# A new operation order for a hybrid transformer block: planner rules and due times changed

## The chip, the cores and the metric

The kernel runs on one core of a Trainium2 chip. The metric is the device time of one execution in microseconds (us); the time before is the median of three runs. A core has five engines that run their own instruction streams side by side: TensorE (PE in the profile, with its weight loads as PEld), VectorE (DVE), ScalarE (ACT), GpSimd (POOL) and SyncE (SP, which here only issues transfers).

## The reference

One layer over 512 tokens of width 1024, all in float32: a norm, one input projection, three groups of attention heads (A: differential attention, 4 heads; B: forgetting attention, 6 heads; C: chunked attention with a relative bias, 6 heads), an output projection into the residual, then a gated MLP with a causal convolution of width 3, and a gated input embedding. Cut to its core:

```python
z = rms_norm(h, ln_mix) @ w_in                       # 1024 -> 3590 columns
q1, q2, k1, k2, va, qf, kf, vf, fg, qc, kc, vc = split(z)
o_a = diff_attention(q1, q2, k1, k2, va, lam, ...)   # softmax - lam * softmax, then a norm per head
o_b = forgetting_attention(qf, kf, vf, log_sigmoid(fg + bias))
o_c = chunk_attention(qc, kc, vc, rel_bias)
h = h + concat(o_a, o_b, o_c) @ w_out
u = rms_norm(h, ln_ffn) @ w_up                       # 1024 -> 2 x 2816
gate, val = split(conv_b + sum(conv_w[j] * shifted(u, j) for j in range(3)))
h = h + (silu(gate) * val) @ w_down
h = h + (p @ w_ple_proj) * sigmoid(rms_norm(h, ln_ple) @ w_ple_gate)
```

## The kernel before

Every float32 product is made of three products of split operands: a matrix is rounded to a high part (`whi`, by ScalarE) and the rest is its low part (`wlo`, mostly by VectorE; some by GpSimd, or by a GpSimd transfer that adds in flight, `wlo<-wraw` on POOL's queue). Weights come from memory into the buffers `wraw` by SP's queue, and in the MLP partly by POOL's, which adds two parts while it loads.

The program has two halves with a plan each: attention (`first`, the class `Plan` with group "first") and the rest (the MLP, its down projection and the gate). The code does not issue an instruction when it is written down. `Plan.add` records it with what it depends on, `Plan.price` gives it a duration, and `Plan.due` gives it a due time: TensorE's operations in the written order follow each other without gaps, and the group that an operation belongs to moves its due time by its entry in the table `SHIFT` (zero when it is absent). Operations of the other engines take their due times from whoever needs them. `Plan.solve` then walks through time: whichever engine can start first takes, among its operations whose inputs are there, the one that is due first. What comes out is the order of instructions on each of the five engines, and `Plan.emit` issues them so; the real waits are semaphores between the engines. A plan's time is a model, and only its order reaches the chip.

Rules of `solve` that matter here:

- TensorE prefers operations whose inputs have been there for `SURE` = 0.1 us.
- A rule on transposes (`turns`, `alone`, `STICK`): TensorE's transposes, through which probabilities, queries, keys and normed tokens pass, are kept in runs. The planner changes between transposes and products only if enough of the other kind is due, and a transpose that stands alone makes the next operation 0.08 us longer.
- Transfers: one `wire` carries SP's and POOL's transfers one after the other.
- `Plan.region` says which bytes an access covers, so that accesses that overlap get a dependency. For the kernel's inputs and output in memory it is one range from the first to the last byte.

Names of groups: `in7_2` is token tile 2 of input projection 7; `B0a` transposes queries and keys of head pair B0, whose halves GpSimd then moves into place (`q<-q`, `q<-ql`, `k<-k`); `B0s0` are the scores of its first head (`s<-k,q`), `B0p0` the transposes of probabilities, `B0v0` the products with the values; `out0_1` is the output projection. In the MLP, `u9_0` is a part of the up projection of column block 9, `s14_1` one of the seven products that a pair of blocks is made of in another way, `dn1_0_t2` a part of the down projection, and `g13_0`, `g13_256` the two halves of the last tile of the gate, whose results go to memory by the last two stores.

The output is made in `kernel` by

```python
    args["out"] = nc.dram_tensor(f"out_{i}_dram", shape, dt, kind="ExternalOutput").ap()[0]
```

All instructions are recorded through one helper, `now`, so that the profile puts them all on one line, L357; the tiles tell them apart.

Of the kernel before, what the change touches and what calls it, by code (L numbers as in the profile page):

```python
# [41 lines left out]
for _i in range(3):  # L42
# [5 lines left out]
AHEAD = 2  # L48
# [46 lines left out]
STAND_INS = {}  # L95
# [28 lines left out]
class Plan:  # L124
# [5 lines left out]
    def __init__(self, clock, there=(), mem=None, fresh=0.0, late=0.0):  # L130
        self.group, self.loaded, self.fresh, self.late = "first", set(), fresh, late
        self.clock, self.there, self.ops, self.mem = clock, [(v.tensor.name, self.region(v), t) for v, t in there], [], mem or {}

    @staticmethod
    def region(v):
        size = 2 if v.dtype == BF16 else 4
        (row, pn), *rest = [tuple(x) for x in v.ap]
        if v.tensor.space == bass.MemoryType.DRAM and v.tensor.name not in STAND_INS:
            return 0, 1, v.offset * size, (v.offset + (pn - 1) * row + sum((n - 1) * st for st, n in rest) + 1) * size
        p0, c0 = divmod(v.offset, row)  # L140
        return p0, p0 + pn, c0 * size, (c0 + sum((n - 1) * st for st, n in rest) + 1) * size
# [42 lines left out]
    def price(self, op):  # L184
# [4 lines left out]
        op.move, op.turns = 0, op.name == "transpose"  # L189
# [29 lines left out]
    LONG, STICK = 0.6, 2.0  # L219
    HW, SW, AT_ONCE = 0.37e6, 0.105e6, 8  # L220
    SURE, AHEAD, MUCH, WAIT = 0.1, 1.0, 2.0, 0.6
# [14 lines left out]
    def solve(self):  # L236
# [6 lines left out]
        wire, out, order = 0.0, {"sp": [], "pool": []}, []  # L243
        turns, alone = False, False
# [4 lines left out]
        while True:  # L249
# [10 lines left out]
            if e == "pe":  # L260
                can = [q for q in can if q.at + self.SURE <= t] or can
            op = min(can, key=rank)
            if e == "pe" and op.turns != turns:
                same = [q for q in can if q.turns == turns and q.dl < op.dl + self.STICK]
# [58 lines left out]
def kernel(ctx: ExitStack, tc: tile.TileContext, x, xt0, xt, pt_in, small, g_ffn_in, bias_c,  # L323
# [15 lines left out]
    PLAN = []  # L339
# [1718 lines left out]
```

## Time and profile before

| | |
|---|---|
| Time, median of 3 runs | 709.2 us (707.82, 709.2, 709.85) |
| Profiled execution | 707.89 us, span 706.0 us |
| TensorE busy | 690.3 us, 98% of the span, 4420 matmuls |
| VectorE busy | 552.5 us, 78%, 1126 instructions |
| ScalarE busy | 408.7 us, 58%, 781 instructions |
| GpSimd busy | 300.6 us, 43%, 403 instructions |
| Transfers | 92.72 MB, mean 131 GB/s |
| Granted TensorE clock | 0.998 |

The span is from the first to the last instruction; the execution takes a little longer than its span. Shares are of the span. An engine that is not on the chain that ended last may stand idle at no cost; TensorE's idle time is what counts in this kernel. A matmul's duration in the profile is modelled and overlaps the next one, so the distance between starts tells more than the durations. Attention fills the first 280 us or so, the up and down projections go on to about 650 us, and the gate ends the kernel.

### The profile page before, as it was taken

The numbers are of one execution on the slowest core, as the hardware profiler recorded it, in microseconds if no ns is written. First come the engines' busy times: TensorE is split into PE (matmuls) and PEld (weight loads), VectorE is DVE, ScalarE is ACT, GpSimd is POOL, SyncE is SP. The second block draws the span as 40 slices with busy tenths as digits, with TensorE's granted clock in tenths as the row PEclk, the third lists the DMA queues.
The fourth block names the chain that finished last, engine by engine and source line by source line (L and its number), as shares of the span: only waits on it lengthen the run. The fifth ranks groups of instructions, "written<-read, shape, count | busy, mean of one in ns | idle before, by whom it ended". The sixth has DMA issues, their size and how long they took to land.

```text
span 706.0 us, 12402 instructions
## 1 busy us (share of the span) xinstructions
PE 690.3 (98%) x4420; PEld 636.4 (90%) x4420; DVE 552.5 (78%) x1126; ACT 408.7 (58%) x781; POOL 300.6 (43%) x403
## 2 busy tenths in 40 slices
PE   7999999999999999999999999999999999999997
PEld 7999999898999888899998999889988888999886
DVE  7679878879788666789888887997877998878722
ACT  6657676565766575666666435665345674536711
POOL 3788677766665452223223334304432203245200
PEclk9999999999999999999999999999999999999999
DMA  9523444423112252584763278651488552204521
GB/s 321 201 83 111 125 117 128 118 60 109 45 61 76 75 124 83 200 244 105 214 159 113 68 186 207 163 162 33 139 211 209 183 168 82 91 32 155 163 85 46
DMA packets 41275, 92.72 MB, mean 131 GB/s; under 512 B 4694, under 2 KB 7510, under 8 KB 41212
## 3 DMA queue, kind: packets, MB, share of 16 engines
q1 hardware_dynamic: 34572, 78.24, 33.1%
q0 software_dynamic: 6352, 13.38, 10.8%
q8 instruction: 35, 0.57, 0.3%
q10 hardware_dynamic: 288, 0.30, 0.1%
q14 instruction: 28, 0.23, 0.1%
HBM read 83.63 MB, written 4.21 MB: 124 GB/s over the span
## 4 chain that ended last, share of the span: by engine, by line
PE 91%; DVE 3%; DMA 2%; ACT 2%; POOL 1%; issue 1%; ACTq 0%; POOLq 0%
PE z L357 46%; PE s L357 22%; PE t L357 16%; PE o L357 7%; DMA wraw<-in_w_up_dram 1%; DVE wlo L357 1%; POOL k L357 1%; POOL q L357 1%; ACT whi L357 1%; DMA zn<-in_w_in_dram 0%; DVE e L357 0%; DVE conv L357 0%; POOL rs L357 0%; ACT e L357 0%; DVE kl L357 0%
## 5 line engine op out<-in xcount | busy, mean ns | idle before, releaser
L357 ACT CAST whi<-wraw 128x768 fp32r<-128x768 f32 (+2 forms) x140 | 106.1, 768 | 59.9 <-POOL wraw L357 11.4
L357 PE MATMUL z<-whi,Th 128*128 128x384 f32 (+2 forms) x356 | 123.4, 351 | 4.5 <-ACT whi L357 4.5
L357 DVE TENSOR_TENSOR wlo<-wraw,whi 128x768 fp32r<-128x768 f32 (+2 forms) x122 | 111.5, 930 | 15.4 <-ACT whi L357 13.6
L357 PE MATMUL z<-wlo,Th 128*128 128x384 f32 (+2 forms) x356 | 123.0, 350 | 0.0
L357 PE MATMUL z<-whi,Tl 128*128 128x384 f32 (+2 forms) x356 | 121.8, 347 | 0.0
L357 PEld LDWEIGHTS z<-whi,Th 128*128 128x128 f32 x356 | 66.9, 189 | 8.0 <-ACT whi L357 4.5
L357 POOL TENSOR_TENSOR wraw<-wraw,wraw 128x256 f32<-128x256 f32 (+1 forms) x22 | 28.3, 1285 | 101.3 <-DVE wlo L357 53.6
L357 PEld LDWEIGHTS z<-wlo,Th 128*128 128x128 f32 x356 | 67.2, 189 | 4.0 <-DVE wlo L357 0.4
L357 PEld LDWEIGHTS z<-whi,Tl 128*128 128x128 f32 x356 | 67.0, 189 | 3.8
L357 ACT ACTIVATE e<-e,st 128x128 f32<-128x128 f32 (+3 forms) x80 | 44.7, 560 | 29.8 <-DVE st L357 29.4
L357 PE MATMUL z<-Th,whi 128*128 128x512 f32 (+1 forms) x156 | 53.2, 346 | 1.4 <-ACT whi L357 1.3
L357 PE MATMUL s<-Th,whi 128*128 128x512 f32 (+1 forms) x156 | 53.3, 345 | 0.6 <-ACT whi L357 0.6
L357 PE MATMUL s<-Th,wlo 128*128 128x512 f32 (+1 forms) x156 | 53.7, 345 | 0.0
L357 PE MATMUL s<-Tl,whi 128*128 128x512 f32 (+1 forms) x156 | 53.6, 345 | 0.0
L357 PE MATMUL z<-Tl,whi 128*128 128x512 f32 (+1 forms) x156 | 53.5, 344 | 0.0
L357 PE MATMUL z<-Th,wlo 128*128 128x512 f32 (+1 forms) x156 | 53.4, 344 | 0.0
L357 POOL TENSOR_TENSOR rs<-rs,nhalf 128x4 f32<-128x4 f32 x40 | 43.5, 1091 | 4.8 <-DVE rs L357 2.3
L357 DVE CUSTOM_DVE_ANT_0 e<-s,bias 128x128 f32<-128x128 f32 (+3 forms) x74 | 33.7, 469 | 12.4 <-PE s L357 7.2
L357 DVE TENSOR_TENSOR conv<-conv,conv 128x512 f32<-128x512 f32 (+1 forms) x31 | 21.0, 691 | 24.0 <-ACT conv L357 23.8
L357 POOL TENSOR_SCALAR e<-e,st 128x512 f32<-128x512 f32 (+3 forms) x48 | 27.2, 576 | 18.1 <-DVE st L357 16.8
L357 PEld LDWEIGHTS z<-Th,whi 128*128 128x128 f32 x156 | 29.1, 188 | 4.8 <-ACT whi L357 1.8
L357 PEld LDWEIGHTS s<-Th,whi 128*128 128x128 f32 x156 | 29.2, 188 | 3.8 <-ACT whi L357 0.8
(352 smaller groups left out, 2152.4 us busy)
## 6 DMA issues: line engine op xcount, KB each, us to landing
wraw<-in_w_up_dram SPq DMA_DIRECT2D x41, 384.0 KB, 4.3
wraw<-in_w_in_dram SPq DMA_DIRECT2D x28, 384.0 KB, 3.7
wraw<-in_w_down_dram SPq DMA_DIRECT2D x16, 384.0 KB, 3.6
whi_again<-in_w_up_dram SPq DMA_DIRECT2D x11, 384.0 KB, 4.5
wraw<-in_w_out_dram SPq DMA_DIRECT2D x16, 256.0 KB, 2.7
wlo_again<-in_w_up_dram SPq DMA_DIRECT2D x10, 384.0 KB, 4.3
wraw<-in_w_up_dram SPq DMA_DIRECT2D x15, 256.0 KB, 4.1
wlo<-wraw POOLq DMA_DIRECT2D x7, 384.0 KB, 4.2
```

Source lines behind the costliest of these rows:

```text
L357: ins = getattr(self.eng, op)(*a, **k)
```

## The change

Five edits, all in the planner; no instruction of the computation is added or removed.

1. The rule on transposes is gone, in both plans: TensorE takes whatever is due first, and a lone transpose has no extra price.
2. The margin `SURE` becomes an argument: 0.15 in attention, 0.1 in the MLP's plan as before.
3. In attention's plan SP's and POOL's transfers have a wire each. The MLP's plan keeps one (`one_wire=True`).
4. `Plan.region` gives a tensor called `out_dram` a rectangle of rows and columns instead of a range of bytes, so that stores to the same rows and other columns do not overlap.
5. The table `SHIFT` has new values throughout, found by a search over the plan; for the MLP the search was made with disturbed landing and operation times.

The lines of `SHIFT` with the groups that the text below speaks of, and the other edits:

```diff
 SHIFT = {
...
-    "in2_1": 19.7, "A0b": -17.1, "in2_2": -18.9, "A0s01": -25, "A0s02": -5.9, "in2_3": -4.1, "fc": 0.8, "in3_0": 4.7,
...
-    "in4_3": 7.8, "in5_0": 4.2, "A1p0": 3.1, "A1s11": -0.2, "in5_1": -10, "A1s12": 2.3, "in5_2": -3.3, "B0a": -0.2,
-    "A1v0": 16.5, "in5_3": -2.8, "A1p1": -3.7, "in6_0": 20.4, "A1v1": -10.3, "B0s0": -8.5, "B0s1": 4, "B1a": -14.7,
...
-    "u9_0": -22.5, "s8_0": -11.8, "u9_1": 7.5, "s8_1": 22.6, "u9_2": 11.4, "s8_6": -22.9, "s8_2": -6.8, "s8_3": -0.9,
...
-    "s14_6": -0.7, "s14_2": 1.3, "s14_3": 5.5, "u17_0": 0.4, "u17_1": -3.4, "s14_4": -0.2, "s14_5": 1.3,
...
-    "g03_0": 10.9, "g10_0": -7.1, "g11_0": -4.4, "g12_0": 1.2, "g13_0": 6.1, "g13_256": 2.2,
...
+    "in1_1": 0.4, "in1_2": -4.5, "A0a": 0.1, "in1_3": -3.6, "in2_0": -0.9, "in2_1": 1, "A0b": 23.2, "in2_2": -4.2,
+    "A0s01": -13.3, "A0s02": -12.2, "in2_3": -2.1, "fc": 21.6, "in3_0": 3.4, "A0p0": -8.9, "A0v0": 8.1, "in3_1": -1,
...
+    "in5_0": 3.3, "A1p0": 19.6, "A1s11": 1.9, "in5_1": 8, "A1s12": -2.6, "in5_2": -0.4, "B0a": -18.4, "A1v0": 7.8,
+    "in5_3": 4.1, "A1p1": -7.9, "in6_0": 0.7, "A1v1": 15.6, "B0s0": -14.1, "B0s1": 7, "B1a": -18.8, "in6_1": -13.2,
+    "B0p0": 8.5, "B0v0": -4.1, "B1s0": -4.4, "in6_2": -1.5, "B0p1": 1, "B1s1": -2.6, "B0v1": -5.6, "B1p0": -0.1,
...
+    "u9_0": 1.7, "s8_0": 24.8, "u9_1": 12.8, "s8_1": -11.8, "u9_2": -20.9, "s8_6": -2.3, "s8_2": -11.8, "s8_3": 1.7,
...
+    "dn1_1_t4": -18.1, "dn1_1_t1": 12.5, "dn1_1_t2": -2.6, "dn1_1_t3": 16.5, "dn1_1_a2": 12, "u15_0": 12.6,
+    "s14_0": -2.1, "u15_1": 14.7, "s14_1": -0.5, "u15_2": -1.5, "s14_2": 5.9, "s14_3": -19.9, "u17_0": -3.4,
+    "u17_1": 0.2, "u17_2": -12.6, "s16_0": 1.4, "s16_2": -6.5, "s16_3": 3.9, "u19_0": -4.1, "u19_1": -0.5,
...
+    "g10_0": -1.8, "g12_0": -7.5, "g13_0": -2, "g13_256": 2.4,
...
-    def __init__(self, clock, there=(), mem=None, fresh=0.0, late=0.0):
+    def __init__(self, clock, there=(), mem=None, fresh=0.0, late=0.0, sure=0.15, one_wire=False):
+        self.sure, self.one_wire = sure, one_wire
         self.group, self.loaded, self.fresh, self.late = "first", set(), fresh, late
         self.clock, self.there, self.ops, self.mem = clock, [(v.tensor.name, self.region(v), t) for v, t in there], [], mem or {}
 
@@ -135,7 +137,7 @@
     def region(v):
         size = 2 if v.dtype == BF16 else 4
         (row, pn), *rest = [tuple(x) for x in v.ap]
-        if v.tensor.space == bass.MemoryType.DRAM and v.tensor.name not in STAND_INS:
+        if v.tensor.space == bass.MemoryType.DRAM and v.tensor.name not in STAND_INS and v.tensor.name != "out_dram":
             return 0, 1, v.offset * size, (v.offset + (pn - 1) * row + sum((n - 1) * st for st, n in rest) + 1) * size
         p0, c0 = divmod(v.offset, row)
         return p0, p0 + pn, c0 * size, (c0 + sum((n - 1) * st for st, n in rest) + 1) * size
@@ -186,7 +188,7 @@
         n = self.width(op.outs[0])
         cols = sum(1 for v in op.ins if self.width(v) == 1) - (op.name == "reciprocal")
         acc = "accum_out" in k
-        op.move, op.turns = 0, op.name == "transpose"
+        op.move = 0
         if e == "pe":
             if op.name == "transpose":
                 op.busy = 0.109
@@ -216,9 +218,9 @@
         op.port = e == "pool" and not op.move or e == "dve" and (
             len(here) == len(op.ins) and (op.name == "tensor_scalar" or op.name in ("tensor_tensor", "scalar_tensor_tensor")))
 
-    LONG, STICK = 0.6, 2.0
+    LONG = 0.6
     HW, SW, AT_ONCE = 0.37e6, 0.105e6, 8
-    SURE, AHEAD, MUCH, WAIT = 0.1, 1.0, 2.0, 0.6
+    AHEAD, MUCH, WAIT = 1.0, 2.0, 0.6
     SPARE = {"act": 1.02, "dve": 1.02, "pool": 1.05}
     ENGINES = ("dve", "pe", "act", "pool", "sp")
 
@@ -240,8 +242,7 @@
             op.left, op.at = len(op.deps), op.ready + self.LEAD[op.eng.name]
             if not op.left:
                 free[op.eng.name].append(op)
-        wire, out, order = 0.0, {"sp": [], "pool": []}, []
-        turns, alone = False, False
+        wire, out, order = {"sp": 0.0, "pool": 0.0}, {"sp": [], "pool": []}, []
         held = {"dve": 0.0, "pool": 0.0}
         other = {"dve": "pool", "pool": "dve"}
         when = lambda q: max(q.at, held[other[q.eng.name]] + (self.late if q.eng.name == "pool" else 0.0)) if q.port else q.at
@@ -258,12 +259,8 @@
             t, e = best
             can = [q for q in free[e] if when(q) <= t]
             if e == "pe":
-                can = [q for q in can if q.at + self.SURE <= t] or can
+                can = [q for q in can if q.at + self.sure <= t] or can
             op = min(can, key=rank)
-            if e == "pe" and op.turns != turns:
-                same = [q for q in can if q.turns == turns and q.dl < op.dl + self.STICK]
-                if same and (turns or sum(q.turns and q.dl < op.dl + self.STICK for q in can) < 2 or min(q.dl for q in same) < op.dl + self.STICK / 2):
-                    op = min(same, key=rank)
             if e not in ("pe", "sp"):
                 soon = [q for q in free[e] if t < when(q) < t + op.busy * self.AHEAD and q.dl < op.dl - self.MUCH]
                 if soon:
@@ -276,15 +273,13 @@
             free[e].remove(op)
             t0 = max(clock[e], when(op))
             busy = op.busy * (1.85 if e == "pe" and t0 < 8.6 else 1.0)
-            if e == "pe":
-                busy += 0.08 * (alone and not op.turns)
-                turns, alone = op.turns, op.turns and not turns
             if op.move:
                 done = out[e]
                 if len(done) >= self.AT_ONCE:
                     t0 = max(t0, done[-self.AT_ONCE])
-                wire = max(t0 + 2.0, wire) + op.move / (self.HW if e == "sp" else self.SW)
-                op.end = wire + 0.6
+                w = "sp" if self.one_wire else e
+                wire[w] = max(t0 + 2.0, wire[w]) + op.move / (self.HW if e == "sp" else self.SW)
+                op.end = wire[w] + 0.6
                 done.append(op.end)
             else:
                 op.end = t0 + busy + op.lag
@@ -1137,7 +1132,7 @@
     for q in ("hi", "lo"):
         pi.tile([P, 768], F32R, tag=f"w{q}", bufs=W[q])
         MORE_RAW.append(pi.again(f"w{q}", W[q], F32))
-    PLAN.append(Plan(first.last, (), first.mem, first.last["dve"] + 0.6, 0.1))
+    PLAN.append(Plan(first.last, (), first.mem, first.last["dve"] + 0.6, 0.1, 0.1, True))
     PLAN[-1].group = "rest"
 
     CONV = 10
```

61 rows, old and new, of the table SHIFT are left out of this document.

## The prediction

> **What bounds the kernel now.** I read the page first (busy time, chain), then TensorE's busy time by stage, then what TensorE waited for, and last the timeline and the DMA issues around each wait.
>
> ```profile
> span 706.0 us, 12402 instructions
> PE 690.3 (98%) x4420; PEld 636.4 (90%) x4420; DVE 552.5 (78%) x1126; ACT 408.7 (58%) x781; POOL 300.6 (43%) x403
> ...
> PE 91%; DVE 3%; DMA 2%; ACT 2%; POOL 1%; issue 1%; ACTq 0%; POOLq 0%
> ```
>
> TensorE (PE) is busy 98% of the span and holds 91% of the chain that ended last. So an order can win only what TensorE stands still. Where that is shows by stage. Each row has the stage, its length, the busy times (and counts) of PE, PE's weight loads, DVE, ACT and POOL, the granted clock, the DMA engines' busy share and GB/s:
>
> ```profile
> 20.00:120.00 100.00, 99.18 (x647) 95.33 (x646) 81.39 (x233) 67.44 (x162) 77.14 (x114) 1.00 0.43 125
> 120.00:165.00 45.00, 41.86 (x255) 38.73 (x253) 36.65 (x126) 27.56 (x68) 29.84 (x42) 1.00 0.38 111
> 165.00:300.00 135.00, 135.00 (x759) 121.24 (x757) 101.33 (x264) 84.55 (x197) 68.18 (x116) 1.00 0.27 87
> ...
> 410.00:420.00 10.00, 9.91 (x81) 9.61 (x81) 7.89 (x11) 3.77 (x5) 3.06 (x3) 1.00 0.59 158
> ...
> 505.00:516.00 11.00, 9.68 (x80) 9.43 (x79) 7.67 (x11) 3.56 (x6) 3.29 (x3) 1.00 0.76 203
> ...
> 540.00:550.00 10.00, 9.43 (x61) 8.37 (x60) 8.27 (x12) 4.14 (x8) 1.72 (x3) 1.00 0.80 221
> ```
>
> Idle is 0.82 + 3.14 us in attention (20 to 300 us) and 0.09 + 1.32 + 0.57 us in the MLP: 4.0 and 2.0. The granted clock is 1.00 in each of these stages. The waits of PE say who ended them (total, times, longest):
>
> ```profile
> PE z L357 <- ACT whi L357: 5.8, 2, 4.5
> PE s L357 <- POOL k L357: 2.1, 3, 1.3
> PE s L357 <- DVE st L357: 1.3, 2, 1.1
> PE s L357 <- ACT whi L357: 0.6, 1, 0.6
> PE t L357 <- DVE kl L357: 0.2, 1, 0.2
> PE t L357 <- DVE ptl L357: 0.2, 1, 0.2
> PE t L357 <- issue: 0.2, 1, 0.2
> ```
>
> The 4.5 us is the start, before the first weights are there, and no order changes it. The other ten waits sum to 1.3 + 2.1 + 1.3 + 0.6 + 3 x 0.2 = 5.9. Idle understates a wait, since a matmul's end is modelled after the point where the next could start:
>
> ```profile
> 513.79 0.28 PE L357 MATMUL t<-Th,wlo 128*128 128x256 f32 x1
> 513.90 0.28 PE L357 MATMUL t<-Th,whi 128*128 128x256 f32 x1
> 515.51 0.50 PE L357 MATMUL z<-Th,whi 128*128 128x512 f32 x1 [1.32 <-ACT whi L357]
> ```
>
> Starts are 0.11 us apart when nothing waits; here 1.61, so 1.50 are lost where 1.32 show, 0.17 more. With 0.17 for each wait, attention loses 4.0 + 8 x 0.17 = 5.4 us and the MLP 2.0 + 3 x 0.17 = 2.5 (its third wait is the 0.09 in 410 to 420). All that an order can take from TensorE is about 7.9 us.
>
> **The change part by part.** No instruction is added or removed: matrix products, splits, copies and loads are the same, and their order on the five queues is computed anew. What each edit can be worth:
>
> *The rule on transposes goes.* It kept transposes together and charged 0.08 us, beside the 0.109 of any transpose, for one that stands alone. One that does:
>
> ```profile
> 30.59 0.27 PE L357 MATMUL t<-ident,zn 128*128 128x128 f32 x1
> 30.61 0.37 PE L357 MATMUL t<-whi,Tl 128*128 128x262 f32 x1
> 30.82 0.29 PE L357 MATMUL t<-whi,Th 128*128 128x262 f32 x1
> 30.94 0.28 PE L357 MATMUL t<-wlo,Th 128*128 128x262 f32 x1
> ```
>
> It and the matmul behind it take 30.82 - 30.59 = 0.23, of which a matmul of this size is 0.12 (30.82 to 30.94): 0.11 for the transpose, the plan's price without the 0.08. So loose transposes cost nothing that shows; at a rounding of 0.01 each, 100 more changes of kind would be at most 1.0 us. I take 0, with 1.0 as the upper end. Gone is also a wrong price by which older orders were judged; what that frees I count with the attention order.
>
> *The attention order (SHIFT of A, B, C, in and out groups; margin 0.15 for 0.1).* Eight waits, 5.4 us. The longest, on POOL's k, begins with one slow copy of q's low part:
>
> ```profile
> 121.78 1.99 POOL q L357
> 123.78 0.59 POOL k L357
> 124.37 0.04 issue
> 124.41 0.74 PE s L357 x4
> ...
> L357 POOL TENSOR_SCALAR q<-ql x20: 611/616/1994, 36.6 to 256.4; 64x512 fp32r<-64x512 f32 x20
> ```
>
> The copy's median is 0.62 us; this one takes 1.99, while VectorE subtracts for wlo: 1.4 us that the plan does not know, and the k that B0s0's scores need stands behind it on POOL. The new shifts set B0a's transposes due 18.2 us earlier (-0.2 to -18.4) and B0s0's scores only 5.6 earlier (-8.5 to -14.1): 12.6 us more room, far over 1.4, so this wait (1.3 + 0.17 = 1.5) should go. B1a and B1s0 both move by about -4 and keep their 0.6. A0b moves 40.3 later (-17.1 to 23.2), A0s01 only 11.7 later: scores that need A0b's k come closer to it, and with them the small wait of POOL's k there may grow by some 0.5. The plan prices operations as before, so slow copies will meet other scores. Estimate from these: 1.0 of 5.4 goes. Ends: all 5.4 gone; or three more meetings of 1.4, +4.2.
>
> *Two wires in the attention plan.* SP's and POOL's transfers no longer delay each other in the plan; the MLP's plan keeps one wire. A load beside a POOL transfer against the median load of this kind:
>
> ```profile
> wlo<-wraw POOLq DMA_DIRECT2D x1, 384.0 KB, 4.9
> wraw<-in_w_in_dram SPq DMA_DIRECT2D x1, 384.0 KB, 4.9
> ...
> wraw<-in_w_in_dram SPq DMA_DIRECT2D x28, 384.0 KB, 3.7
> ```
>
> They do delay each other: 4.9 for 3.7, 1.2 us. What hides it now is that loads run ahead: none of the attention waits above ends with a transfer. I take 0; if the cover is gone, 1.2 for each such load. The Trainium skill (Trainium Kernel Development and Optimization, Key Constraints) says that DMAs from SP, ACT and POOL run on the same 16 engines and interleave. The trace agrees, and the rule speaks against this edit; with the 1.2 of the row above for five loads the sum below would end 6.0 higher, a rival below.
>
> *The MLP order (SHIFT from u0 on).* All three waits end with a split of weights that landed late. Their loads, and those of a quiet stretch:
>
> ```profile
> 413.51 4.27 DMA wraw<-in_w_up_dram
> ...
> 538.98 5.21 DMA wraw<-in_w_up_dram
> ...
> wraw<-in_w_up_dram SPq DMA_DIRECT2D x2, 384.0 KB, 8.3
> wlo_again<-in_w_up_dram SPq DMA_DIRECT2D x1, 384.0 KB, 6.6
> ...
> conv<-in_w_down_dram SPq DMA_DIRECT2D x3, 256.0 KB, 2.6
> ```
>
> From 507 to 511 us loads go out together and take 6.6 to 8.3 us; alone, at 580 to 589, 2.6. By the order of the groups, u9_0, u15_0 and u17_1 waited. Their shifts go from -22.5 to 1.7, from 0 to 12.6 and from -3.4 to 0.2: each is due later by 24.2, 12.6 and 3.6 us, more than the 0.3, 1.5 and 0.7 that it waited. Whole groups move with their loads, and SP issues in order, so one load that waits for a free buffer holds all behind it and makes a new burst for another unit. I take 2.5 to 0.8, one wait of the mean size: -1.7. Ends: -2.5, and twice the waits, +2.5.
>
> *The stores' regions.* The edit asks for a tensor called out_dram; the output is created as out_0_dram, so it does nothing. What it aims at is there:
>
> ```profile
> 700.57 0.42 DVE L357 TENSOR_TENSOR conv<-conv,h 128x256 f32<-128x256 f32 x1
> ...
> 701.76 0.42 DVE L357 TENSOR_TENSOR conv<-conv,h 128x256 f32<-128x256 f32 x1
> 702.21 0.81 SPq L357 DMA_DIRECT2D out_dram<-conv  x2
> ```
>
> One half is ready at 700.99 and yet both stores are issued back to back from 702.21 on (0.81 for two): the plan queues g13_0's store first, and g13_0 is the half that is ready last. The new shifts turn this round without the edit (g13_0 6.1 to -2, g13_256 2.2 to 2.4): g13_0 ends first, its store leaves at once, and the last one saves half of 0.81: -0.4 (ends 0 and -0.4).
>
> **Sum.** -1.0 (attention) + 0 (transposes) + 0 (wires) - 1.7 (MLP) - 0.4 (tail) = -3.1 us. The profiled execution took 707.89 us (span 706.0 and 1.9 around it) and would take 704.8. It is at the fast end of the runs shown (707.82 to 709.85); I put the same difference to their median: 709.2 - 3.1 = 706.1. The ends sum to -8.3 and to +7.7.
>
> **The rivals.**
> *Waits only move* (no change). Every wait is a meeting that the plan did not foresee, and prices are the old ones. For: the 1.99 copy is no term of the plan. Against: the three MLP waits have one cause, and their units got room. With only the tail gained: 708.8.
>
> *POOL and VectorE meet more often* (slower). Place: 40 to 165 us, where POOL is busy most (77.14 of 100, 29.84 of 45). Each meeting in front of scores costs 1.4. With the 2.1 of MLP and tail kept, three cost as much as is won twice over: -2.1 + 4.2 = +2.1, 711.3; from three more on it is slower. Against: q<-ql shows one such maximum, and 165 to 300 us has no idle at all.
>
> *Loads late by two wires* (slower). Each uncovered load beside a POOL transfer costs 1.2. Against the sum of -3.1 that is no change with three or four, and slower by over 2.1 from the fifth on: -3.1 + 6.0 = +2.9, 712.1. Against: no wait of attention ends with a load now, so the cover is there. The Trainium skill's rule on the 16 engines, above, describes this case.
>
> **How the numbers follow.** A measurement of this kernel tells about 0.3% (2.1 us) from no change. Forecast 0.52 (706.1, its own range 703.0 to 707.0); waits only move 0.30; meetings 0.13; wires 0.05. Faster 0.52, same 0.30, slower 0.18. The range reaches from 703.0, below which more than two thirds of all idle would have to go, to 711.2, just short of the two slower cases: about 1 in 10 is left out at either end.
>
> **What would show it.** Right: PE's waits between 300 and 700 us under 1.0 in sum, no wait of B0s0 on POOL's k above 0.5, transposes in more and shorter runs at 0.11 each, the two last stores issued about 1.2 us apart, instruction counts unchanged. Wrong: a DMA in the chain of attention (wires); POOL copies of 1.5 us and more ahead of score matmuls (meetings); a burst of loads over 7 us with a split and a PE wait behind it (MLP order).

## The result and the profile after

The changed kernel took 702.47 us (median of 701.65, 702.4, 702.55 and 702.68) against 708.51 for the kernel before beside it: a ratio of 0.9912, interval 0.9891 to 0.9933. Against the 706.1 that was forecast it is 3.6 faster, and 0.5 below the low end of the range. Of the 3.6, 0.7 is the base: the forecast started from 709.2, and the kernel before took 708.51 beside this one. The change itself is -6.0 for the -3.1 forecast. The profiled execution took 701.65 us; its span of 699.9 is 6.1 below the 706.0 of before.

The page of the changed kernel, its lines on span, engines and chain:

```profile
span 699.9 us, 12389 instructions
PE 690.2 (99%) x4420; PEld 636.2 (91%) x4420; DVE 554.4 (79%) x1126; ACT 409.9 (59%) x781; POOL 293.8 (42%) x403
...
PE 97%; POOL 1%; DMA 0%; DVE 0%; ACT 0%; issue 0%; POOLq 0%
```

The five engines have the same counts of instructions as before, and PE's busy time is the same (690.2 for 690.3). What went is its idle time: PE now holds 97% of the chain instead of 91%. Its waits, all of them, then the six stages that the prediction showed of before:

```profile
PE z L352 <- ACT whi L352: 4.5, 1, 4.5
PE t L352 <- DVE zn L352: 0.2, 1, 0.2
```

```profile
20.00:120.00 100.00, 99.91 (x662) 95.92 (x661) 84.92 (x244) 67.24 (x162) 72.79 (x111) 1.00 0.45 124
120.00:165.00 45.00, 44.74 (x270) 42.07 (x269) 36.71 (x127) 31.45 (x76) 29.78 (x45) 1.00 0.27 73
165.00:300.00 135.00, 135.00 (x755) 120.31 (x755) 102.61 (x258) 84.74 (x196) 69.79 (x114) 1.00 0.35 104
410.00:420.00 10.00, 10.00 (x86) 10.00 (x86) 8.70 (x16) 3.73 (x6) 2.68 (x4) 1.00 0.90 208
505.00:516.00 11.00, 11.00 (x86) 10.55 (x84) 10.04 (x18) 4.37 (x8) 2.09 (x3) 1.00 0.96 250
540.00:550.00 10.00, 10.00 (x59) 8.73 (x58) 9.11 (x16) 6.09 (x10) 3.15 (x4) 1.00 0.75 190
```

The 4.5 is the start; apart from it a single wait of 0.2 is left where there were ten of 5.9 in sum. In the MLP TensorE has no idle time in any of the three stages, though transfers are denser there than before: 0.90 for 0.59 of the DMA engines in 410 to 420 us, 0.96 for 0.76 in 505 to 516. In 120 to 165 us it gained 2.88 (44.74 for 41.86), in 20 to 120 us 0.73.

Idle time hides part of a wait, so the comparison below counts starts: the distance from each matmul of the trace to the next, less the usual distance for its width (0.109 us at 128 columns, 0.118 at 256, 0.175 at 384, 0.233 at 512), summed by stage. What is left is the loss. The distances are rounded to a thousandth, and 2,700 matmuls stand behind 300 us: with the distances exactly as given here, that column reads about 0.8 higher in every row, the others up to 0.25 higher. So the columns serve to compare the kernels. The last column is the time from the last matmul's start to the end of the span. This table holds the kernels that the experiments below compare:

| loss in us | 0–20 | 20–120 | 120–140 | 140–165 | 165–300 | 300–700 | end |
|---|---|---|---|---|---|---|---|
| before | 1.36 | 3.00 | 3.07 | 1.86 | 0.39 | 2.44 | 5.54 |
| after | 1.77 | 2.22 | 0.62 | 0.99 | 0.81 | -0.06 | 5.11 |
| att_new | 2.57 | 2.10 | 0.61 | 1.03 | 2.28 | 1.38 | 5.51 |
| mlp_order | 1.55 | 2.82 | 3.06 | 1.85 | 0.44 | -0.10 | 4.67 |
| old_one_move_b | 1.81 | 2.83 | 2.15 | 1.87 | 0.43 | 0.96 | 5.54 |
| old_two_moves_b | 1.40 | 2.83 | 2.16 | 1.03 | 0.48 | 1.83 | 5.53 |

From before to after: attention (20 to 300 us) 8.32 to 4.64, so -3.7; the MLP -2.5; the end -0.4; the start +0.4, which lies between 1.3 and 2.9 in every kernel and follows no edit. The sum is -6.2, against 6.1 by the spans. Attention's pattern is the same to 0.2 in kernels that share its order (before and mlp_order), so its losses come with the order. The old MLP order loses a different amount in each profile (2.44, 0.96 and 1.83), the new one the same in both (-0.06 and -0.10); where the new order stands in after_more, tail_old and new_with_rule below, TensorE has no idle time from 300 to 690 us either.

The end, in the timeline after (the row of SP holds both stores, 0.33 each, so the second begins 1.67 behind the first):

```profile
694.38 0.42 DVE L352 TENSOR_TENSOR conv<-conv,h 128x256 f32<-128x256 f32 x1
...
694.83 2.00 SPq L352 DMA_DIRECT2D out_dram<-conv  x2
...
696.05 0.42 DVE L352 TENSOR_TENSOR conv<-conv,h 128x256 f32<-128x256 f32 x1
```

The two last stores go out at 694.83 and 696.50, each 0.03 behind its addition, instead of both together behind the second.

From the last matmul's start to the landing of the last store it is 3.46 us (694.77 to 698.23), for 3.95 before (700.48 to 704.43): 0.49 less. What follows the landing are the program's closing semaphores and drains, and their length varies: 1.65 after, 1.59 before and 1.21 in mlp_order, whose two stores land exactly as in the changed kernel (3.46). The 4.67 of that row is no further gain of the order.

### The profile page after: what moved, and what is told of

The parts are those of the page before. It is cut to its first block, busy times and chain, and to the rows that moved or that the text cites. A ratio compares the mean times of both kernels' runs of the same rounds, so it can differ in the third digit from the quotient of the medians.

```text
span 699.9 us, 12389 instructions
## 1 busy us (share of the span) xinstructions
PE 690.2 (99%) x4420; PEld 636.2 (91%) x4420; DVE 554.4 (79%) x1126; ACT 409.9 (59%) x781; POOL 293.8 (42%) x403
## 4 chain that ended last, share of the span: by engine, by line
PE 97%; POOL 1%; DMA 0%; DVE 0%; ACT 0%; issue 0%; POOLq 0%
PE z L352 50%; PE s L352 22%; PE t L352 18%; PE o L352 7%; DMA zn<-in_w_in_dram 0%; POOL e L352 0%; POOL rs L352 0%; POOL wlo L352 0%; DVE conv L352 0%; DVE oall L352 0%; ACT otmp L352 0%; ACT whi L352 0%; DVE zn L352 0%; ACT conv L352 0%; ACT ptc L352 0%
## 5 line engine op out<-in xcount | busy, mean ns | idle before, releaser
L352 DVE TENSOR_TENSOR wlo<-wraw,whi 128x768 fp32r<-128x768 f32 (+2 forms) x122 | 109.4, 911 | 14.5 <-ACT whi L352 14.1
L352 PE MATMUL z<-Tl,whi 128*128 128x512 f32 (+1 forms) x156 | 52.0, 345 | 0.0
L352 POOL TENSOR_SCALAR e<-e,st 128x256 f32<-128x256 f32 (+3 forms) x48 | 29.2, 643 | 10.2 <-DVE st L352 8.2
L352 PEld LDWEIGHTS s<-Tl,whi 128*128 128x128 f32 x156 | 29.2, 188 | 3.3
```

Source lines behind the costliest of these rows:

```text
L352: ins = getattr(self.eng, op)(*a, **k)
```

## The experiments

The kernels with old tables or with the old rule come from one planner that has the rule as an argument of each plan. Theories are numbered afresh in each expectation.

**Half by half.** The new attention with the old MLP table and rule (att_new):

```diff
-    "u9_0": 1.7, "s8_0": 24.8, "u9_1": 12.8,
+    "u9_0": -22.5, "s8_0": -11.8, "u9_1": 7.5,
...
-    PLAN.append(Plan(first.last, (), first.mem, first.last["dve"] + 0.6, 0.1, 0.1, True))
+    PLAN.append(Plan(first.last, (), first.mem, first.last["dve"] + 0.6, 0.1, 0.1, True, rule=True))
```

> Attention with its new order (new due times, no rule on transposes, margin 0.15, two wires), the MLP with the old due times and the old rule. Theory 1 (each half's order removes its own waits): from the starts of TensorE's instructions the new kernel lost 3.3 us less before 300 us, 2.5 less after it, and 0.4 less behind the last matmul; so this one gains 3.3 of the 6.0 us, about 705.2 against 708.5, and TensorE waits in attention as little as in the changed kernel (0.2 us of idle) while the MLP's waits of some 2 us come back. Theory 2 (the waits are chance meetings that any new order deals anew): waits of either half change without a pattern; attention's sum could be anything from 0.2 to 4.

Measured 705.42, ratio 0.9957 (0.994 to 0.9974). What TensorE waited for:

```profile
PE z L360 <- ACT whi L360: 4.8, 3, 4.4
PE z L360 <- DVE h L360: 1.0, 1, 1.0
PE t L360 <- DVE zn L360: 0.2, 1, 0.2
```

The waits on POOL's k and on st are gone with the attention order alone. A new one of 1.0 stands at the junction of the halves (280 to 300 us), where the old MLP table meets another state than it was made for. For the same reason the MLP's order is not quite the old one: its matmuls stand as in the kernel before only from 372 us on, and the 2 us of waits that were expected to come back did not (0.5 of idle from 300 to 690 us). So the 3.2 us under the 708.58 beside it are a sum. By the table, 20 to 165 us lose 4.2 less than before (4.1 less in the changed kernel), the junction 1.9 more and the MLP 1.1 less.

The opposite, old attention and the new MLP table with the rule off there (mlp_new):

```diff
-    "u9_0": -22.5, "s8_0": -11.8, "u9_1": 7.5,
+    "u9_0": 1.7, "s8_0": 24.8, "u9_1": 12.8,
...
-    PLAN.append(Plan(first.last, (), first.mem, first.last["dve"] + 0.6, 0.1, 0.1, True, rule=True))
+    PLAN.append(Plan(first.last, (), first.mem, first.last["dve"] + 0.6, 0.1, 0.1, True))
```

> The old attention order, the MLP with the new due times and without the rule. Theory 1: gains 2.5 in the MLP and 0.4 at the end, about 705.6; attention's idle of 4.0 us stays, the MLP's is under 0.3. Theory 2: MLP waits of 1 to 3 us at other places, about 708.

Measured 713.44, ratio 1.0079 (1.0054 to 1.0104): slower. In the MLP (second row) TensorE is idle 6.1 us, for 2.0 before:

```profile
20.00:300.00 280.00, 275.92 (x1659) 255.35 (x1659) 221.17 (x624) 180.20 (x428) 174.47 (x268) 1.00 0.36 104
300.00:690.00 390.00, 383.87 (x2572) 350.16 (x2571) 311.61 (x460) 211.63 (x326) 116.70 (x118) 1.00 0.52 142
```

The planner, started a little differently, put the operations in another order: of some 2,700 matmul rows of the MLP only about the last 1,050 stand as in the changed kernel. So this run did not test the new order. The next one did: the old attention, and the MLP's order of the changed kernel written down operation by operation (mlp_order):

```diff
+ORDER = {
+    "rest": [
...
-        return self.solve()
+        order = self.solve()
+        PLANS.append(self)
+        which = "attention" if len(PLANS) % 2 else "rest"
+        return [self.ops[p] for p in ORDER[which]] if which in ORDER else order
```

> The old attention order, and behind it the MLP's operations in exactly the order of the changed kernel, instruction by instruction, written down instead of computed (with the new due times the planner had made another MLP order behind the old attention). Theory 1 (the order itself carries the gain): the MLP loses nothing again, 2.5 us less, and the end 0.4 less, so about 705.7 against 708.6, with under 0.4 us of TensorE idle between 300 and 650 us. Theory 2 (chance, or only in step with the attention before it): MLP waits of 1 us and more return, 707 to 709.

Measured 704.88, ratio 0.9952 (0.9938 to 0.9965), 3.0 us under the 707.86 beside it. The two stages:

```profile
20.00:300.00 280.00, 276.19 (x1661) 255.41 (x1660) 220.32 (x623) 180.22 (x427) 175.50 (x270) 1.00 0.36 104
300.00:690.00 390.00, 390.00 (x2618) 357.50 (x2617) 313.65 (x465) 213.87 (x327) 115.06 (x119) 1.00 0.52 144
```

No idle in the MLP; attention as before (3.81 idle). With att_new's 3.2 us the halves sum to 6.2, near the 6.0 of the whole change, though att_new is not attention alone, as said above.

The changed kernel once more, unedited, in five rounds (after_more):

> The changed kernel again, unaltered, in more runs beside the kernel before. If its order tolerates what varies from run to run (landing times above all), its times lie within some 1.5 us (the first four: 701.65 to 702.68), where those of before spread over 5.5 us (706.18 to 711.74). If the profiled run was only a lucky one, the times spread as widely as before's, up to 707.

Measured 702.6, ratio 0.9922 (0.9909 to 0.9934). Its nine executions lie between 701.65 and 703.22, these five between 702.52 and 703.22. The nine of the kernel before beside them lie between 707.33 and 709.35, and fourteen beside att_new between 706.18 and 711.74. The spread goes with the MLP's order: att_new, with the old MLP table, takes 704.47 to 707.19, and mlp_order 704.5 to 704.97.

**The rule on transposes.** The kernel before with the rule off in attention's plan alone (old_no_rule, the first pair of lines), and the changed kernel with the rule on there (new_with_rule, the second pair):

```diff
-    PLAN.append(Plan({...}, (...), sure=0.1, one_wire=True, rule=True))
+    PLAN.append(Plan({...}, (...), sure=0.1, one_wire=True))
...
-    PLAN.append(Plan({...}, (...)))
+    PLAN.append(Plan({...}, (...), rule=True))
```

> Only the rule on transposes is taken out of attention's plan; due times, margin and wire are the old ones. If the rule itself held attention back (more choice for TensorE): faster by 1 to 3 us, 706 to 707. If the gain is in the due times that were searched for the planner without the rule: no gain, 708 to 712, since the old due times fit a planner with the rule; the number of transpose runs rises from 67 to over 100 in any case, at no cost of its own (0.11 us for each transpose, alone or not).

> The changed kernel with the rule on transposes put back into attention's plan alone. If the rule costs time as such: slower than the changed kernel by 1 to 3 us, with TensorE waits ahead of transposes. If only the match of due times and planner counts: also slower, by as much as old_no_rule is against before, and the waits stand anywhere. If neither matters: within 0.7 us of 702.5. The MLP's waits stay under 0.5 us in each case.

Measured 734.96, ratio 1.0376 (1.0343 to 1.0409), and 725.65, ratio 1.0241 (1.0208 to 1.0274). Attention loses 33 and 27 us from 20 to 300 us (8.3 and 4.6 with the rules that belong to the tables): in these two pairs a table is worth something only with the rule under which it was searched. The transposes stand in 85 and 91 runs here, fewer than the 100 expected of the first. That says nothing on what a transpose costs; the changed kernel's own trace does. Its 312 transposes stand in 137 runs instead of 67, each takes 0.11 from start to start, and the excess over the usual distances at the changes of kind has a median of under 0.01 us.

All due times of the changed kernel moved at random by up to 1 us either way (jitter1):

```diff
-    "in1_1": 0.4, "in1_2": -4.5, "A0a": 0.1, "in1_3": -3.6,
+    "in1_1": -0.3, "in1_2": -3.8, "A0a": 0.6, "in1_3": -4.1,
...
```

> The changed kernel with every due time moved at random by up to 1 us either way. If the table stands for orders that are good as a kind (the planner without the rule, times searched with room): within 3 us of 702.5, waits under 2 us in sum. If only the exact order is good, as the runs with half-matching tables suggest (713 to 735 us): 10 to 30 us slower, with waits all over both halves.

One execution: 741.38, a span of 739.6. This one draw of a table that is off by 1 us at most ends 33 us above the kernel before (708.3 beside it) and 39 above the changed kernel. How other draws come out was not run.

**Is the new order more tolerant?** Both kernels with extra work that changes nothing computed: three memsets of 64 columns by GpSimd ahead of each of the 60 copies of q and k, and a transfer of 256 KB within memory behind every second transfer of SP in the MLP (noisy_old, noisy_new):

```diff
+            if self.one and op.eng.name == "pool" and op.name == "tensor_scalar" and self.width(op.outs[0]) == S and op.outs[0].shape[0] == HD:
+                EXTRA[0]()
             op.ins = op.eng.now(op.name, [real(v) for v in op.a], {q: real(v) for q, v in op.k.items()})
+            if not self.one and op.eng.name == "sp" and op.name == "dma_start":
+                EXTRA[1]()
```

> The kernel before in its own order, disturbed twice: in attention three memsets of 0.15 us each on POOL ahead of each of its 60 copies of halves of q and k (26 us of POOL work more), in the MLP plan a further transfer of 256 KB, from memory to memory, behind every second transfer of SP. The result is the same, these are extra. Expected of it: TensorE's idle in attention from 4.0 to some 12 us, in the MLP from 2.0 to some 8; about 722.

> The changed kernel with the same two disturbances. Theory 1 (the new MLP order, searched with disturbed landings, tolerates late loads better): TensorE idles 2 to 3 us in the MLP where the disturbed old one idles about 8; attention, searched without, loses as much as the old one, some 8 us more: about 713. Theory 2 (no more tolerant, it only meets fewer late events undisturbed): the disturbance costs both kernels the same in both halves within a third, so the gap between them stays about 6 us.

Measured 743.12, ratio 1.0501 (1.0471 to 1.0531), and 737.26, ratio 1.0407 (1.0383 to 1.0431): 20 to 25 us more than expected of each. Over the whole kernel the disturbance costs the two the same, 35.3 us over the 707.86 of the kernel before beside it and 34.7 over the 702.6 of the changed one. They differ in where it is lost. The longest sum of waits and the MLP's stage, the old order first:

```profile
PE s L364 <- POOL k L364: 17.5, 9, 3.2
```

```profile
300.00:690.00 390.00, 383.20 (x2585) 350.25 (x2584) 316.89 (x472) 215.65 (x335) 119.26 (x127) 1.00 0.65 192
```

```profile
PE s L359 <- POOL k L359: 21.8, 10, 4.9
```

```profile
300.00:690.00 390.00, 388.71 (x2625) 356.35 (x2624) 321.54 (x477) 223.25 (x346) 121.84 (x133) 1.00 0.67 197
```

In the MLP the same disturbance (the DMA engines busy for 0.65 and 0.67 of the time) leaves 6.8 us idle in the old order, 4.8 more than undisturbed, and 1.3 in the new: that order bears extra transfers better. In attention both lose much, the new order rather more (21.8 for 17.5 on POOL's k; 22.6 us of idle in all, for 21.4). Attention's gain is therefore not tolerance.

**Attention's meetings.** VectorE's subtract and GpSimd's copy stand in each other's way in the kernel before at 122 us, and VectorE's two subtracts and GpSimd's own at 155 us; timeline rows of before:

```profile
121.78 1.99 POOL L357 TENSOR_SCALAR q<-ql 64x512 fp32r<-64x512 f32 x1
122.36 0.94 DVE L357 TENSOR_TENSOR wlo<-wraw,whi 128x768 fp32r<-128x768 f32 x1
...
155.05 3.91 DVE L357 TENSOR_TENSOR wlo<-wraw,whi 128x768 fp32r<-128x768 f32 x2
155.98 2.15 POOL L357 TENSOR_TENSOR wlo<-wraw,whi 128x768 fp32r<-128x768 f32 x1
...
158.88 0.34 DVE L357 CUSTOM_DVE_ANT_0 e<-s,fbias,st 128x128 f32<-128x128 f32 x1
```

The first trials moved only VectorE's subtracts behind the score evictions that TensorE waits for (old_one_move the first of them, old_two_moves both). A moved subtract there reads its source after the reload and so splits another tile of weights: these two kernels leave out the order between a subtract and the reload of its source, and their result is not the layer's.

```diff
-        return self.solve()
+        order = self.solve()
+        PLANS.append(self)
+        for what, behind in MOVES if len(PLANS) % 2 else ():
+            order.remove(self.ops[what])
+            order.insert(order.index(self.ops[behind]) + 1, self.ops[what])
+        return order
```

> The kernel before with one instruction moved: VectorE's subtract for wlo that ran from 122.36 to 123.30 us now stands four places later on VectorE's queue, behind the second score eviction of B0s0 (its first reader is in in7, some 25 us later). Theory 1 (attention's waits are meetings of VectorE's and POOL's operations that the order makes, the same in every run): POOL's copy of q's low part falls from 1.99 us to about 0.62, the scores' wait of 1.3 us on POOL's k goes, and the smaller waits behind it (0.36, 0.40, 0.55) shrink: 1.3 to 1.9 us faster. Theory 2 (POOL is simply behind by then, and the copy's length does not matter): the wait moves to the next scores, within 0.5 us of before.

> That move, and a second: of two VectorE subtracts for wlo that took 3.83 us together from 155.13 on, with POOL's own subtract of 2.15 us beside them, the second stands behind the score evictions of B1s1. Theory 1: the wait of 1.1 us on VectorE ahead of B1s1's scores goes as well, 2.5 to 3.1 us faster than before, which is nearly all of the 3.3 us that the new attention order gains. Theory 2: within 0.7 us of before.

Measured 707.61, ratio 0.9983 (0.9968 to 0.9999), and 709.06, ratio 1.0013 (0.9996 to 1.003). With both moved, both meetings went, but the second moved subtract had to wait for the reload of its source, held VectorE's queue, and made a new wait, `PE o <- ACT otmp`, of 2.2 us. So the same moves were made again with the reload behind the subtract (old_one_move_b, old_two_moves_b). The two pairs of `MOVES`, an operation and the one that it goes behind, became four (old_one_move_b has the first two):

```diff
-MOVES = ((1676, 1345), (1953, 1582))
+MOVES = ((1676, 1345), (1948, 1676), (1953, 1582), (2221, 1953))
```

> The kernel before; one subtract of VectorE that makes wlo (the one that stood beside GpSimd's slow copy of q at 122 us) goes four places down VectorE's queue, behind the second score eviction of B0s0, and the load that refills its source stays behind it. Theory 1 (attention's gain is the end of two single meetings): GpSimd's longest q<-ql falls from 1.99 to about 0.65, the wait of B0s0 on GpSimd's k from 1.3 to under 0.3, TensorE's loss in 120 to 140 us by 0.9 to 1.5; time 0.9 to 1.5 us under the kernel before (ratio 0.998 to 0.9987). Theory 2 (the gain is looseness of the whole new order, and a meeting taken away comes back elsewhere): GpSimd's next operation is slow in its place, and the time is the same within 0.3 us.

> As old_one_move_b, and a second subtract, the one beside which GpSimd's own subtract took 2.15 us at 155 us, goes behind the score eviction that B1s1 waits for; the load that refills its source goes with it, past two other loads of SP. Theory 1: the wait of B1s1 on VectorE's st (1.1) goes too, and the loss in 140 to 165 us falls by about 1.4; time 2.3 to 2.9 us under the kernel before (ratio 0.996 to 0.9968), most of the 3.3 us that attention gained. Theory 2: the second gain does not show; time within 0.3 us of old_one_move_b.

Measured 706.63, ratio 0.998 (0.9968 to 0.9992), and 706.25, ratio 0.997 (0.9959 to 0.9981), that is 1.3 and 1.7 us under the 707.93 beside them. The rows of old_one_move_b for the first meeting, and of old_two_moves_b for the second:

```profile
122.02 0.61 POOL L365 TENSOR_SCALAR q<-ql 64x512 fp32r<-64x512 f32 x1
...
124.26 0.95 DVE L365 TENSOR_TENSOR wlo<-wraw,whi 128x768 fp32r<-128x768 f32 x1
```

```profile
154.24 0.98 DVE L365 TENSOR_TENSOR wlo<-wraw,whi 128x768 fp32r<-128x768 f32 x1
155.17 2.15 POOL L365 TENSOR_TENSOR wlo<-wraw,whi 128x768 fp32r<-128x768 f32 x1
156.39 0.35 DVE L365 CUSTOM_DVE_ANT_0 e<-s,fbias,st 128x128 f32<-128x128 f32 x1 [1.17 <-PE t L365]
```

The copy takes 0.61 instead of 1.99, and VectorE reaches the score eviction behind the second meeting at 156.39 instead of 158.88, now with 1.17 to spare. TensorE's waits on POOL's k fall from 2.1 (longest 1.3) to 0.8 (longest 0.4). By the table of losses, 120 to 140 us gives back 0.92 and 140 to 165 us 0.84. Nearly half of attention's 3.7 can thus be had by ending two single meetings, each by moving one subtract and the reload behind it. The first move gave what was expected of it (0.9 to 1.5 us). Both together gave 1.7 where 2.3 to 2.9 was expected: part of the second gain goes into a new wait at 162 us, `PE o <- ACT otmp` again (0.4 of idle, 0.58 by the starts). The second ratio lies 0.001 under the first, and their intervals overlap, so 0.84 rests on the traces. What the rest is made of was not taken apart: another 1.5 in 120 to 140 us, where old_two_moves_b still has four gaps of 0.30 to 0.56 ahead of scores and transposes, and 0.6 in 20 to 120 us.

**The end.** The changed kernel with the old due times of g13_0 and g13_256 (tail_old):

```diff
-    "g10_0": -1.8, "g12_0": -7.5, "g13_0": -2, "g13_256": 2.4,
+    "g10_0": -1.8, "g12_0": -7.5, "g13_0": 6.1, "g13_256": 2.2,
```

> The changed kernel with the two due times of the last tile's halves set back (g13_0 to 6.1, g13_256 to 2.2). If the order of these halves is what the end gains: the last two stores are issued back to back again and the time from the last matmul's start to the end of the span goes from 5.1 back to 5.5 us; TensorE's work is the same. If the stores' order does not matter: 5.1 stays.

One execution: 702.83, a span of 701.1. The stores stand back to back again:

```profile
697.19 0.81 SPq L352 DMA_DIRECT2D out_dram<-conv  x2
```

From the last matmul's start to the end it takes 5.60, for 5.11 in both profiles of the changed kernel, and to the landing of the last store 3.94 for 3.46: 0.5 us, by the order of the halves alone.

## Why the prediction was only partly right

The direction, the places of the gains and the tail held. The size was forecast at half, -3.1 for -6.0, because the prediction let waits come back in other places, most of attention's and a third of the MLP's, and they did not.

*Attention, -1.0 forecast, -3.7 found.* The failed step is "The plan prices operations as before, so slow copies will meet other scores. Estimate from these: 1.0 of 5.4 goes." That is 1.5 for the wait of B0s0 less 0.5 for A0's; the other waits were left to stand or to come back. The wait of B0s0 on POOL's k went as forecast, and A0's did not grow. But the others went too, and no new one took their place. Slow operations there still are, in the changed kernel's rows of the copy:

```profile
L352 POOL TENSOR_SCALAR q<-ql x20: 612/614/1299, 35.6 to 246.8; 64x512 fp32r<-64x512 f32 x20
```

One copy still takes 1.30 (1.99 before), with no wait on POOL's k anywhere. Nor are meetings rarer on the whole. Of GpSimd's operations from 20 to 283 us, 24 take over 0.3 us more than the median of their form, 13.6 us more in sum; before there were 21, with 14.4 (GpSimd's spans are rough). So slow operations do meet others, as the step says, but TensorE waits behind one chain of them only, for the 0.2 us on `zn` at 131 us. Meetings are no chance that strikes a share of all orders: the losses repeat in kernels that share an order (before and mlp_order), so an order found by search can have none in front of TensorE.

The prediction also misread the plan when it called the slow copy "no term of the plan". In `solve` of both kernels an operation with `port` set (GpSimd's own, and VectorE's subtracts for wlo among others) starts only when the other engine's operation with `port` is over (`held`). A search over the plan therefore sees meetings, as waits. What it doesn't see is a start that comes a little otherwise on the chip: in the kernel before the subtract began at 122.36, 0.58 behind the copy, which usually takes 0.61. Which of the two the plan had put first, no run shows.

By the prediction's own measure (idle and 0.17 for each wait) attention went from 5.4 to 0.35 + 0.17 = 0.5, that is by 4.9 where the starts give 3.7. That measure leaves out starts that come late without idle time; they sum to about 2.8 us before and 3.5 after.

*MLP, -1.7 forecast, -2.5 found, and -3.0 with the end in mlp_order.* The failed step is "one load that waits for a free buffer holds all behind it and makes a new burst for another unit. I take 2.5 to 0.8". The bursts remain: the DMA engines are busy for 0.96 of 505 to 516 us, and the three loads of 384 KB from SP to `wraw` that are in flight from 503 to 518 us land in 6.3 us in the median (7.8 before). No unit waits for them. The noisy pair fits an order that leaves more room between a load and its use; that room itself was not measured. That a table by itself is no guarantee shows in mlp_new, with 6.1 us of idle in an order made from the same due times.

*Held:* transposes at 0; two wires at 0 (no wait of attention ends with a DMA); the stores 0.4, by the due times, 1.67 apart where 1.2 was expected. That the edit of the regions does nothing was not run by itself, but mlp_order has the old `region` and its two stores stand 1.67 apart all the same, and tail_old accounts for them by the due times. The two wires and the margin of 0.15 were not run by themselves either: what they did to attention's order is not told apart from the table.

*The rivals.* No change and both slower ones did not come. Waits that only move are real all the same: with tables that do not fit, the same planner gives 713 to 741 us, with the waits at other places.

## What to carry to other kernels

An order found by search belongs to the planner and the state that it was searched with: to carry it over, or to test half of it, write the order down literally instead of its due times. A search that disturbs landing times gave an MLP order here that lost less to extra transfers (1.3 us for 6.8) and spread less. Two engines that slow each other at one place are worth a look in the timeline: moving one instruction, and the reload that depends on it, took away 0.8 to 0.9 us each time by the traces.

## What the runs showed of the hardware

*A long wait can cost more than its length.* Waits of 1.3 us left the granted clock of the kernel before at 1.00. Rows of TensorE's timeline in jitter1, and stretches of 4 us there with the granted clock in the third column from the end:

```profile
182.75 0.47 PE L352 MATMUL o<-pth,V 128*128 128x512 f32 x1 [0.81 <-DVE oall L352]
183.35 0.49 PE L352 MATMUL o<-ptl,V 128*128 128x512 f32 x1
186.46 0.69 PE L352 MATMUL z<-whi,Th 128*128 128x384 f32 x1 [2.62 <-DVE zn L352]
...
188.22 0.52 PE L352 MATMUL z<-whi,Tl 128*128 128x384 f32 x1
188.54 0.52 PE L352 MATMUL z<-whi,Th 128*128 128x384 f32 x1
...
192.29 0.34 PE L352 MATMUL z<-whi,Tl 128*128 128x384 f32 x1
192.46 0.34 PE L352 MATMUL z<-whi,Th 128*128 128x384 f32 x1
```

```profile
180.00:184.00 4.00, 2.33 (x12) 1.28 (x10) 3.29 (x6) 1.39 (x4) 3.84 (x4) 1.00 0.83 189
184.00:188.00 4.00, 1.54 (x5) 1.54 (x6) 0.97 (x2) 0.00 (x0) 2.70 (x4) 0.62 0.63 197
188.00:192.00 4.00, 4.00 (x15) 4.00 (x14) 0.00 (x0) 0.00 (x0) 0.00 (x0) 0.53 0.00 0
192.00:196.00 4.00, 4.00 (x25) 4.00 (x24) 0.00 (x0) 0.04 (x1) 0.00 (x0) 1.00 0.00 0
```

From the end of the wait of 2.62 at 186.46 to 191.74 matmuls of 384 columns start 0.32 apart; from 192 on, with the clock back at 1.00, 0.17. That is some 16 matmuls and 2.4 us on top of the wait. Stretches at this pace make up some 12 of the 45 us that jitter1 loses behind the first 10 us, and some 5 of 34 in old_no_rule. The Trainium skill (TensorE: Matmul & The Clock Gate, Part 1: The HAM clock gate) says that an idle window of about 3.4 us drops the clock to half and a busy one restores it. The trace agrees with the half: 0.53 from 188 to 192 us, and 0.5 in its clock record from 184.96 to 191.79. The clock was thus down 1.1 us into the wait of 2.62, and an idle window in full was not needed: in the 3.41 us before, TensorE stood still for 2.1. In the 16 drops ahead of the kernel's end that jitter1, old_no_rule, new_with_rule and the noisy pair show together, these 3.41 us held 1.6 to 3.4 us of idle time, and the clock stayed at half for 3.41 or 6.83 us. One wait of 2.2 us at 156 us in old_no_rule left it at 1.00.

*GpSimd and VectorE shut each other out.* GpSimd's copy of 0.61 us took 1.99 beside VectorE's subtract of 0.94; two such subtracts took 3.91 beside GpSimd's 2.15, where one alone takes 0.98. The Trainium skill (SBUF — State Buffer, Who interferes with whom) calls the ports that the two share an exclusive lock. The trace agrees: the copy that began at 121.78 ended at 123.77, behind the subtract's end at 123.30. Here the one that gave way was the copy, though it had begun first, as far as GpSimd's rough spans tell.
